# Writing the first stage's order by hand: TensorE, GpSimd and SyncE in program order, two recurrences interleaved

## The chip, the cores and the metric

The kernel runs on one core of one Trainium2 chip. The metric is device time in microseconds (us) of one execution, the median over several executions; lower is better. The engines of the core are named as the profile names them: PE is TensorE's matmul, PEld its weight loads, DVE is VectorE, ACT is ScalarE, POOL is GpSimd and SP is SyncE, which here only issues DMA transfers. An engine takes its instructions in the order in which they stand in its queue, so an instruction that waits holds back all that stand behind it on that engine.

## The reference

The reference is a two-layer decoder trunk on x of 1 x 1024 x 1024 in float32. Layer 0 mixes tokens with an HGRN2 gated recurrence, layer 1 with a causal convolution module; each is followed by a squared-ReLU MLP, and each of the four parts by a layer norm of the scaled residual. The change touches layer 0's mixer alone:

```python
proj = h @ w_in                                   # (S, 4D): q | forget | value | output gate
q, fz, v, g = jnp.split(proj, 4, axis=-1)
q = silu(q);  f = lb + (1 - lb) * sigmoid(fz);  k = 1 - f
# 8 heads of 128 x 128, chunkwise over time:
#   S_t = diag(f_t) S_{t-1} + k_t v_t^T,   o_t = S_t^T q_t
o = o * rsqrt(mean(o * o, -1) + RMS_EPS) * norm_g * silu(g)
mix = o @ w_out
```

## The kernel before

**Numbers and products.** Every large product is made of float32 operands cut into a high and a low part (ACT casts the high one, DVE subtracts to get the low one; `cut`, L348), so a product of two operands is three matmuls: high-high, high-low, low-high. On top of that the projections use a seven-product scheme for 2 x 2 blocks in place of eight. The products are numbered 1 to 7 and run in the order 1, 2, 6, 5, 7, 3, 4 (`ORDER`, L43). Each needs its own sum of input blocks and its own sum of weight blocks, called forms.

**The first stage** is layer 0's mixer up to the output projection, and has these parts.

- *Value products* (`v_products`, L399): seven products, each of four token tiles with 12 matmuls of 512 columns. The order in the program is 1, 2, 6, 5, 7, 3, 4. The forms of x and of the value weights are made in between by DVE, ACT and POOL from five buffers `x00` to `x11` and `t6`, and `a0` to `a3` and `s7`. Finished values go to `vd` in device memory (L397).
- *Pair products* (`pair_product`, L729): twelve pairs, `PAIRS` in L513. A "q" pair makes Q and the forget gate of one head, a "g" pair the output gates of two heads. A pair is seven products of 12 matmuls, so there are 12 x 7 x 12 = 1008 of them. `pair_load` (L515) brings a pair's weights in two transfers into the one buffer pair `r0`, `r1`, and `pair_forms` (L523) makes its seven weight forms: POOL adds the blocks (L532 to L539), ACT and DVE cut the sums into a ring `fs` of eight slots. The forms of pair p+1 are made while pair p is multiplied, and as soon as they are made `pair_load(p + 2)` is issued (L549).
- *Recurrences* (`recurrence`, L572): one for each head and half of the sequence, sixteen in all. Each one is a chain that goes back and forth between DVE and PE: DVE multiplies Q and K by running decay products (`grow`, L593) at seven levels, POOL makes a rescaled copy `kd` (L610), PE makes scores at these levels into PSUM, DVE merges them under masks (`put`), PE transposes K, then multiplies scores by values and carries the state over four blocks, with a DVE step between. ACT takes squares, POOL the power -1/2 of the mean square (`power_m_half`, L428), ACT scales, PE transposes, and the result is stored to `od` (L695). `recurrence` is a generator; each `yield` ends a step.
- *Gates*: `swish` (L701) multiplies on POOL; `gate_out` (L770) loads a head from `od`, multiplies it by its gate on POOL, and stores it to `zd`.
- *Output projection* (from L1007): eight products of 24 matmuls for each half, from tiles `oT`, which `gated` and `last_head` fill, and weights `wb` and `wa`.

**Weight sums for later.** The MLPs use the seven products too. The sums of blocks of `ffn_w2` are made during the first stage, entirely by transfers in device memory: `block_sums` (L489) issues on SP a tiny store that serves as a gate on a computed tile (L493) and two loads of 1 MB (L494, L495), and then on POOL's queue three accumulating transfers, each of which must wait until what it adds to has landed:

```python
nc.gpsimd.dma_start(out=v[:, 0:2], in_=w[:, 2:4], accum_op=ALU.add)                                  # L496
for i in (2, 3):
    nc.gpsimd.dma_start(out=v[:, i], in_=v[:, i - 1], accum_op=ALU.add, max_dma_last_dim=4096)       # L498
```

There are sixteen such sums. Each of the first two recurrences starts two of them, each of the next ten starts one (L684), all when its normed output is there; the last two run in layer 1.

**What sets the order.** The program emits the work in one order: after each pair product so many steps of the oldest recurrence (`advance`, L754; 16/7 a product, 24/7 in the second and the last pair), one recurrence at a time, then the gates that are ready. This emission order is a priority only. A planner simulates the engines and puts each engine's queue, those of PE, POOL and SP included, in the order in which, by its own cost model, instructions become ready. On the chip each queue then runs as it was written.

The loop over the pairs, L861 to L881, shortened:

```python
for p, (kind, j) in enumerate(PAIRS):
    forms = None if last else pair_forms(p + 1)
    for i in ORDER:
        if kind == "q" and i == 2:
            while recs and recs[0][0] <= j - 2:      # Q and K have four slots
                advance()
        pair_product(p, i, made.pop(0), st)          # twelve matmuls
        next(forms)                                  # one form of the next pair
        rate += (24 if p in (1, len(PAIRS) - 1) else 16) / 7
        while rate >= 1:
            rate = rate - 1 if advance() else 0.0    # one step of the oldest recurrence
        gate_some()
    if kind == "q":
        recs += [[j, 0, None], [j, 1, None]]
```

Most PE and DVE instructions are issued through a helper at L172, so the profile shows that line for them and they are told apart by their tiles: `ps<-vw,xf` is a value product, `ps<-xf,fs` a pair product, `qk`, `kd`, `at`, `state`, `v`, `ident,o` belong to recurrences, `wa,oT` and `wb,oT` to the output projection, `raw` is a pair's weight buffer and `s` its form 7, `ss` is the mean square, `sum_w` a weight sum.

Of the kernel before, what the change touches and what calls it, by code (L numbers as in the profile page):

```python
# [236 lines left out]
def body(ctx, tc, d, out):  # L237
# [100 lines left out]

    par = cst.tile([P, NPAR], F32, name="par")
# [7 lines left out]

    def cut(hi, lo, raw):  # L348
        nc.scalar.copy(out=hi, in_=raw)  # L349
        vector.tensor_tensor(out=lo, in0=raw, in1=hi.bitcast(F32), op=ALU.subtract)  # L350
# [4 lines left out]
    def form_v(i):  # L355
        at = {1: (80, 88), 2: (96, 104), 6: (192, 200), 5: (208, 96), 7: (192, 200), 3: (208, 184), 4: (192, 200)}[i]
        VS[i] = [view(kb, (2, 1024), F32R, "vw") for kb in at]
# [41 lines left out]
    def v_products(i):  # L399
        for t, parts in enumerate(v_form(i)):  # L400
            product(banks[:, 4 + t] if i in (2, 5, 3) else banks[:, t], parts, i in (1, 2, 5))
            v_out(i, t)

# [12 lines left out]
    products([banks[:, t] for t in range(NTB)], v_form(1))  # L416
    load_v(a2, 1, 0)
    load_v(a3, 1, 2)
    load_x(x01, 1, 0)
# [19 lines left out]
    pool_add(s7[:, 0], a0[:, 0], a2[:, 0])  # L439
    for j in range(2):  # L440
        if j:
            vector.tensor_tensor(out=s7[:, j], in0=a0[:, j], in1=a2[:, j], op=ALU.add)
        for o, x, y in ((a2, a2, a3), (a0, a2, a0)):
            if j:
                vector.tensor_tensor(out=o[:, j], in0=x[:, j], in1=y[:, j], op=ALU.add)
            else:
                pool_add(o[:, j], x[:, j], y[:, j])
    for k in range(4):
        vector.tensor_tensor(out=x00[:, k], in0=x00[:, k], in1=x01[:, k], op=ALU.subtract)
        vector.scalar_tensor_tensor(out=t6[:, k], in0=x00[:, k], scalar=-1.0, in1=x11[:, k], op0=ALU.mult, op1=ALU.subtract)  # L450
        cut_x(6, t6, (k,))
    cut_v(6, a0)
    v_products(2)

    cut_x(5, x00)
    cut_v(5, a2)
    for k in range(4):
        vector.scalar_tensor_tensor(out=x10[:, k], in0=t6[:, k], scalar=-1.0, in1=x10[:, k], op0=ALU.mult, op1=ALU.subtract)
        pool.tensor_tensor(out=x01[:, k], in0=x11[:, k], in1=x01[:, k], op=ALU.subtract)
    outs_v(5)  # L460
# [3 lines left out]
    cut_x(3, x11)  # L464
    outs_v(4)
    lg = par[:, LB : LB + H]
# [9 lines left out]
    pool_add(a1[:, 0], a0[:, 0], a1[:, 0])  # L476
    vector.tensor_tensor(out=a1[:, 1], in0=a0[:, 1], in1=a1[:, 1], op=ALU.add)
    v_products(5)

    cut_x(7, x01)  # L480
    cut_v(7, s7)
    v_products(7)
    cut_v(3, a1)
    cut_x(4, x10)


    sums = {}

    def block_sums(name, layer, c, after):  # L489

        t = sums[name, layer, c] = dram.tile([4, P, 1024], F32, name=f"sum_{name}{layer}{c}")
        v, w = t.rearrange("a p n -> p a n"), d[name][layer, c].rearrange("a p n -> p a n")
        nc.sync.dma_start(out=t[0:4:2, 0, 0:1], in_=after)  # L493
        nc.sync.dma_start(out=v[:, 0:2], in_=w[:, 0:4:2])  # L494
        nc.sync.dma_start(out=v[:, 2:4], in_=w[:, 0:2])  # L495
        nc.gpsimd.dma_start(out=v[:, 0:2], in_=w[:, 2:4], accum_op=ALU.add)  # L496
        for i in (2, 3):
            nc.gpsimd.dma_start(out=v[:, i], in_=v[:, i - 1], accum_op=ALU.add, max_dma_last_dim=4096)  # L498

    to_sum = [(*of, c) for of in (("w2", 0), ("w2", 1)) for c in range(NFC)]  # L500

    def form(name, layer, c, i):

        w, t = d[name][layer, c], sums[name, layer, c]
        return {1: w[0], 2: w[1], 6: t[2], 5: t[1], 7: t[0], 3: t[3], 4: w[3]}[i]


# [58 lines left out]
    def load_values(i):  # L566
        if i < 2 * H:
            h, half = divmod(i, 2)
            vts[i] = view(166, rows, F32, "v") if i == 2 * H - 1 else vs()
            nc.sync.dma_start(out=vts[i], in_=vd[h // 4][half][:, :, h % 4 * P : (h % 4 + 1) * P])  # L570

    def recurrence(h, half):  # L572
# [4 lines left out]
        state = carry if half else None  # L577
# [11 lines left out]
        def total(n):  # L589
            t = totals[n].rearrange("p (b s) -> p s b", s=2)  # L590
            mul(totals[2 * n], t[:, 0], t[:, 1])

        def grow(n, k=True):  # L593
            nb = HT // (2 * n)
            if not k:
# [38 lines left out]
        for n in (16, 32, 64):  # L634
# [9 lines left out]
            if n == 16:  # L644
                put(0, pd)
# [211 lines left out]
    for _ in forms:  # L857
        pass
# [698 lines left out]
```

## Time and profile before

| | |
|---|---|
| median of 3 executions | 2360.37 us (2360.34 to 2363.32) |
| the profiled execution | 2359.79 us, its span 2358.0 us |
| granted clock over the span | 0.951 |
| PE busy | 2169.4 us (92%) |
| DVE, ACT, POOL busy | 1466.4, 1040.2, 547.6 us |
| mean DMA rate | 216 GB/s |

A profile is one execution. Busy time is the time in which at least one instruction of an engine ran; matmuls are pipelined, so the time between the starts of two matmuls that follow each other is what one costs, and it is shorter than the mean duration that a group shows. The granted clock is the share of TensorE's full speed that the chip let it have. A wait is put down to the instruction, or the transfer, that ended it.

### The profile page before, as it was taken

Reading aid. Unit: us, or ns where it says so; the run is one execution under the profiler, and the core shown is the slowest. Engines: PE = TensorE matmul, PEld = TensorE weight load, DVE = VectorE, ACT = ScalarE, POOL = GpSimd, SP = SyncE. Lnnn points to the kernel's source line nnn. Section 1 sums busy time; section 2 is a strip of 40 time slices with the busy share of each in tenths; the row PEclk is TensorE's granted clock in tenths of the full one; section 3 lists DMA queues with packets and bytes.
Section 4 is the critical chain, followed back from the end, with each engine's and each line's share of the span. In section 5 each row is a group of like instructions: output and inputs, shape, how many; then the busy total and the mean of one; then the engine's idle time right before and its main releaser. Section 6 shows DMA issues by size and latency. Waiting matters only on the chain.

```text
span 2358.0 us, 27326 instructions
## 1 busy us (share of the span) xinstructions
PE 2169.4 (92%) x10056; PEld 1787.7 (76%) x10056; DVE 1466.4 (62%) x1938; ACT 1040.2 (44%) x1607; POOL 547.6 (23%) x458
## 2 busy tenths in 40 slices
PE   7996486786779999999999999999999999999998
PEld 5875365565668888888888888888887888888887
DVE  8584355373547776665665679978963654455446
ACT  5342132242421465555444447664854344343333
POOL 3242433343211000000000028937920100000001
PEclk8997788797889999999999999999999999999999
DMA  4317965756713377768999986556459598875552
GB/s 167 104 53 200 219 179 142 188 145 166 209 47 135 115 254 243 280 214 297 359 337 345 328 303 234 180 215 232 171 180 326 183 339 318 299 262 192 194 177 99
DMA packets 170951, 508.63 MB, mean 216 GB/s; under 512 B 16192, under 2 KB 45120, under 8 KB 169792
## 3 DMA queue, kind: packets, MB, share of 16 engines
q1 hardware_dynamic: 161856, 473.32, 57.3%
q0 software_dynamic: 8960, 33.56, 8.1%
q8 instruction: 79, 1.29, 0.2%
q14 instruction: 56, 0.46, 0.1%
HBM read 377.32 MB, written 196.61 MB: 243 GB/s over the span
## 4 chain that ended last, share of the span: by engine, by line
PE 68%; DMA 15%; DVE 6%; POOL 5%; issue 3%; ACT 2%; SPq 0%; DVEq 0%; POOLq 0%
PE ps L172 68%; DMA sum_w<-in_w_dram 4%; DMA raw<-in_wqf_dram 3%; POOL cb L172 2%; DVE qk L172 2%; DMA raw<-in_w_dram 1%; DMA sum_w<-sum_w 1%; DMA y<-kept 1%; DMA wa<-ready 1%; DVE fs L172 1%; DMA vr<-in_wv_dram 1%; DMA dh<-hf 1%; POOL ss L429 1%; DMA raw<-in_wg_dram 1%; POOL kd L172 1%
## 5 line engine op out<-in xcount | busy, mean ns | idle before, releaser
L172 PE MATMUL ps<-dw,dh 128*128 128x512 f32 x2688 | 611.3, 389 | 0.5 <-ACT dh L69 0.5
L172 PEld LDWEIGHTS ps<-dw,dh 128*128 128x128 f32 x2688 | 504.1, 188 | 105.4 <-ACT dh L69 0.9
L172 PE MATMUL ps<-x1f,fw 128*128 128x512 f32 x1344 | 307.9, 390 | 1.0 <-DVE c L172 1.0
L172 PEld LDWEIGHTS ps<-x1f,fw 128*128 128x128 f32 x1344 | 251.4, 188 | 53.1 <-issue 1.4
L172 PE MATMUL ps<-xf,fs 128*128 128x512 f32 x1008 | 269.5, 427 | 21.2 <-ACT t L736 19.5
L172 PE MATMUL ps<-xa,wa 128*128 128x512 f32 x1152 | 268.8, 392 | 0.0
L172 PEld LDWEIGHTS ps<-xf,fs 128*128 128x128 f32 x1008 | 205.7, 208 | 69.8 <-ACT t L736 21.1
L172 PEld LDWEIGHTS ps<-xa,wa 128*128 128x128 f32 x1152 | 214.3, 188 | 43.5
L172 POOL TENSOR_TENSOR cb<-cb,prod 128x512 f32<-128x512 f32 x176 | 234.2, 1340 | 17.7 <-ACT prod L1325 7.2
L172 DVE TENSOR_TENSOR dh<-dh 128x1024 fp32r<-128x1024 f32 x112 | 136.4, 1222 | 118.9 <-ACT dh L69 117.0
L172 DVE SCALAR_TENSOR_TENSOR ps<-u,par,ps 128x512 f32<-128x512 f32 x288 | 198.7, 750 | 9.8 <-ACT ps L1337 8.4
L429 POOL TENSOR_TENSOR mv<-mv,nhalf 128x1 f32<-128x1 f32 x32 | 47.4, 1483 | 655.5 <-DVE mv L172 655.5
L172 DVE TENSOR_TENSOR dw<-dr,dw 128x1024 fp32r<-128x1024 f32 x112 | 136.6, 1222 | 100.8 <-ACT dw L69 100.4
L69 ACT CAST dh<-dh 128x1024 fp32r<-128x1024 f32 x112 | 117.0, 1051 | 150.0 <-DMA dh<-hf 147.0
L69 ACT CAST dw<-dr 128x1024 fp32r<-128x1024 f32 x112 | 117.4, 1053 | 132.1 <-PE ps L172 115.1
L172 PE MATMUL ps<-xc,wa 128*128 128x512 f32 x768 | 174.4, 389 | 0.0
L172 PEld LDWEIGHTS ps<-xc,wa 128*128 128x128 f32 x768 | 144.1, 188 | 29.9
L1325 ACT ACTIVATE prod<-u,par 128x512 f32<-128x512 f32 x176 | 125.3, 722 | 54.0 <-POOL cb L172 53.4
L1190 POOL COPY next<-ss 128x1 f32<-128x1 f32 x37 | 15.9, 429 | 488.5 <-DVE spare L172 235.1
L172 DVE TENSOR_TENSOR qk<-qk,T 128x512 f32<-128x512 f32 x96 | 73.0, 762 | 89.4 <-PE ps L172 53.4
L349 ACT CAST fs<-raw 128x512 fp32r<-128x512 f32 x72 | 44.0, 619 | 173.6 <-POOL raw L172 67.5
L172 DVE TENSOR_TENSOR fs<-raw,fs 128x512 fp32r<-128x512 f32 x72 | 64.6, 902 | 87.5 <-ACT fs L349 86.9
(193 smaller groups left out, 2986.7 us busy)
## 6 DMA issues: line engine op xcount, KB each, us to landing
wa<-ready SPq DMA_DIRECT2D x122, 512.0 KB
dh<-hf SPq DMA_DIRECT2D x112, 512.0 KB
ready<-spare SPq DMA_DIRECT2D x74, 512.0 KB
sum_w<-in_w_dram SPq DMA_DIRECT2D x32, 1024.0 KB
dr<-sum_w SPq DMA_DIRECT2D x64, 512.0 KB
raw<-in_w_dram SPq DMA_DIRECT2D x51, 512.0 KB
dr<-in_w_dram SPq DMA_DIRECT2D x48, 512.0 KB
raw<-in_w1q_dram SPq DMA_DIRECT2D x36, 512.0 KB
```

What stands on the lines that cost most here:

```text
L69: self.nc.scalar.copy(out=slot[:, 0, c], in_=raw[:, c])
L172: return op(*args, **kw)
L349: nc.scalar.copy(out=hi, in_=raw)
L429: nc.gpsimd.tensor_tensor(out=dst, in0=src, in1=nhalf[:, :n], op=ALU.pow)
L1190: nc.gpsimd.tensor_copy(out=raw[:, :1], in_=now)
L1325: nc.scalar.activation(tp, u[:, k : k + HT], AF.Copy, scale=tap(j, k))
```

## The change

PE, POOL and SP leave the planner for the whole first stage: their queues run in the order in which the program emits the work (`tc.manual_schedule`). DVE and ACT stay with the planner, and so does everything after the stage. The emission order is rewritten to go with it:

- The value products run in the order 1, 2, 5, 6, 7, 3, 4, with the forms made right ahead of each; `x01` is loaded ahead of `a2` and `a3`.
- A clock of ticks is kept: one tick after every three matmuls of a pair product or of the early output products, four after a tile of a value product. `later(n, job)` emits a job n ticks later. A weight sum's two loads are emitted at once, its three accumulating transfers 24, 48 and 72 ticks later.
- The first four sums start in value products 5, 6, 7 and 3, one in each; the first ten recurrences start one each. As before, two are left for layer 1.
- A pair product is emitted in quarters of three matmuls. After each quarter, from the second pair on, 222/308 of a recurrence step is emitted. Two recurrences are under way at a time: the next starts when the one before has made seven of its fourteen steps. The state updates and the last steps are spread over more steps than before, and the state passes between the halves of a head through `carry`, kept by head.
- `kd` and the product in Q's swish go from POOL to DVE. In the g pairs the swish of a copied gate stays on POOL.
- The forms are made at most five products ahead, in a ring of six slots in place of eight; Q and K get six slots in place of four.
- A gate's multiplication on POOL is emitted six ticks after its load is issued.
- At the end of the stage three output products, (0,0), (1,0) and (2,0), are made in the last steps of the last recurrence; the five others of the first half follow after the stage, in another order than before.

The core of the diff:

```diff
+    order = ExitStack()
+    order.enter_context(tc.manual_schedule(engines={mybir.EngineType.PE, mybir.EngineType.Pool, mybir.EngineType.SP}))
...
+    def later(n, job):
+        if n:
+            waiting.append((ticks[0] + n, job))
+        else:
+            job()
+
+    def tick(n=1):
+        for _ in range(n):
+            ticks[0] += 1
+            for at, job in [w for w in waiting if w[0] <= ticks[0]]:
+                waiting.remove((at, job))
+                job()
...
+    def block_sums(name, layer, c, after, gap=0):
...
+        nc.sync.dma_start(out=t[0:4:2, 0, 0:1], in_=after)
+        nc.sync.dma_start(out=v[:, 0:2], in_=w[:, 0:4:2])
+        nc.sync.dma_start(out=v[:, 2:4], in_=w[:, 0:2])
+        parts = [lambda: nc.gpsimd.dma_start(out=v[:, 0:2], in_=w[:, 2:4], accum_op=ALU.add)]
+        for i in (2, 3):
+            parts.append(lambda i=i: nc.gpsimd.dma_start(out=v[:, i], in_=v[:, i - 1], accum_op=ALU.add, max_dma_last_dim=4096))
+        for i, part in enumerate(parts):
+            later((i + 1) * gap, part)
...
     def v_products(i):
...
             v_out(i, t)
+            if t == 0 and i in (5, 6, 7, 3):
+                block_sums(*to_sum.pop(0), VO[{5: 5, 6: 6, 7: 5, 3: 6}[i]][0][:2, :1], 24)
+            tick(4)
...
     def recurrence(h, half):
...
-        pool.tensor_tensor(
-            out=kd.rearrange("p a (b n) -> p a b n", n=4), in0=B.rearrange("p a (b n) -> p a b n", n=4),
-            in1=cutout(rm, 0, [[P, 2], [1, P], [0, 4]]), op=ALU.mult,
-        )
+        mul(kd.rearrange("p a (b n) -> p a b n", n=4), B.rearrange("p a (b n) -> p a b n", n=4), cutout(rm, 0, [[P, 2], [1, P], [0, 4]]))
...
-        for _ in range(2 if 2 * h + half < 2 else 1 if 2 * h + half < 12 else 0):
-            block_sums(*to_sum.pop(0), o[:2, 0, :1])
+        if 2 * h + half < 10:
+            block_sums(*to_sum.pop(0), o[:2, 0, :1], 24)
+        yield
         yield
...
-            pool.tensor_tensor(out=out, in0=t, in1=sg, op=ALU.mult)
+            (vector if out is not t else pool).tensor_tensor(out=out, in0=t, in1=sg, op=ALU.mult)
...
     def pair_product(p, i, f, st):
...
+        for k in range(4):
...
+            tensor.matmul(ps, lh, rh, start=i in (1, 2, 5) and k == 0, stop=False, **group)
+            tensor.matmul(ps, lh, rl, start=False, stop=False, **group)
+            tensor.matmul(ps, ll, rh, start=False, stop=k == 3, **group)
+            if k < 3:
+                slot()
...
+        slot()
...
+    def step():
+        if recs and (not active or len(active) == 1 and active[0][2] >= 7):
+            at = recs.pop(0)
+            active.append([at, recurrence(*at), 0])
+        if not active:
+            return False
+        one = active[0]
+        if len(active) == 2 and active[0][2] - active[1][2] > 7:
+            one = active[1]
+        one[2] += 1
...
+    def slot():
+        tick()
+        pace[0] += pace[1]
+        while pace[0] >= 1:
+            pace[0] = pace[0] - 1 if step() else 0.0
...
+        pending.append(rest)
+        later(6, lambda: pending and pending[0] is rest and pending.pop(0)())
...
     for p, (kind, j) in enumerate(PAIRS):
...
+        pace[1] = 222 / 308 if p else 0.0
...
+    early_out = ((0, 0), (1, 0), (2, 0))
+    for (t, n), ps in zip(early_out, (banks[:, i] for i in range(3))):
+        for k, ((lh, ll), (rh, rl)) in enumerate(wide(oT[0], t, ws[n])):
...
+            tick()
+            if k % 2:
+                step()
+    while step():
+        pass
+    gated(1, range(H - 2))
     last_head(1)
+    tick(100)
...
+    order.close()
```

283 lines of the change are left out of this document (131 added, 152 removed).

## The prediction

> **What bounds the kernel now.** I read the slices of the page first, to see where TensorE (PE) is idle, then the chain that ended last, then tables by stage, then the groups and waits of the stage.
>
> ```profile
> span 2358.0 us, 27326 instructions
> PE   7996486786779999999999999999999999999998
> PEclk8997788797889999999999999999999999999999
> PE 68%; DMA 15%; DVE 6%; POOL 5%; issue 3%; ACT 2%; SPq 0%; DVEq 0%; POOLq 0%
> ```
>
> A slice is 59 us. Slices 3 to 12 are ragged in both rows, everything after is 9: the loss lies in the first stage, to about 712 us. A fifth of the chain is DMA and GpSimd (POOL), engines that should hide.
>
> ```profile
> 50.00:75.00 25.00, 25.00 (x112) 20.69 (x111) 17.62 (x29) 12.65 (x20) 0.00 (x0) 1.00 0.08 23
> 97.00:712.00 615.00, 453.47 (x2343) 368.63 (x2342) 326.43 (x536) 188.18 (x431) 208.29 (x158) 0.83 0.59 150
> 125.00:175.00 50.00, 46.08 (x224) 36.74 (x225) 43.48 (x66) 19.86 (x35) 21.88 (x15) 0.97 0.14 43
> 712.00:850.00 138.00, 137.04 (x663) 114.17 (x662) 104.91 (x149) 50.59 (x87) 12.86 (x9) 1.00 0.40 140
> 91.78 5.60 PE L172 MATMUL ps<-vw,xf 128*128 128x512 f32 x24
> 97.22 3.11 PE L172 MATMUL ps<-xf,fs 128*128 128x512 f32 x13
> ```
>
> The stretch table gives PE, weight loads, VectorE (DVE), ScalarE (ACT) and POOL busy, granted clock, DMA share, GB/s; below are two rows of the timeline. The value (V) products end and the pair products begin at 97. From 97 to 712 (615 us) PE is busy for 453 at a clock of 0.83; after 712 it is busy for 137 of 138. At full clock PE takes 25.00 / 112 = 0.223 us per 512-column matmul. Its real work in the 615 us follows from the groups:
>
> ```profile
> L172 PE MATMUL ps<-xf,fs 128*128 128x512 f32 x1008 | 269.5, 427 | 21.2 <-ACT t L736 19.5 <-DVE t L172 1.0 <-DVE fs L172 0.4
> L172 PE MATMUL ps<-qk 128*128 128x128 f32 x256 | 44.9, 331 | 21.2 <-DVE qk L172 14.6 <-ACT on L691 6.5
> L172 PE MATMUL ps<-wa,oT 128*128 128x512 f32 x49 | 16.3, 469 | 2.7 <-ACT wa L69 1.9 <-DVE wa L172 0.8
> L172 PE MATMUL ps<-ident,o 128*128 128x128 f32 x60 | 14.3, 361 | 51.1 <-ACT o L683 51.1
> L172 PE MATMUL ps<-wb,oT 128*128 128x512 f32 x48 | 13.0, 402 | 3.2 <-DVE oT L172 2.7 <-DVE t L172 0.6
> L172 PE MATMUL ps<-qk 128*32 128x32 f32 x256 | 7.5, 204 | 7.0 <-DVE qk L172 7.0
> 640.18 1.05 PE L172 MATMUL ps<-qk 128*128 128x128 f32 x8
> 648.73 0.45 PE L172 MATMUL ps<-qk 128*32 128x32 f32 x16
> 654.98 0.68 PE L172 MATMUL ps<-qk 128*64 128x64 f32 x8
> ```
>
> Pair products: 1008 x 0.223 = 225 us. Recurrences: seven 128-column groups, from x256 to x56, hold 852 matmuls at 1.05 / 8 = 0.131, so 112; 256 narrow ones at 0.45 / 16 make 7, 128 half-wide ones at 0.68 / 8 make 11; together 130. The 97 output-projection matmuls already inside are 22. That is 377 us of work in 615: **238 us are lost to waits and half clock**, the most the change can win there. Who causes the waits:
>
> ```profile
> L498 POOL DMA_DIRECT2D sum_w<-sum_w x28 | 24.0, 858 | 125.5 <-DMA sum_w<-in_w_dram 80.0 <-DMA sum_w<-sum_w 45.5
> L496 POOL DMA_DIRECT2D sum_w<-in_w_dram x14 | 17.2, 1230 | 95.3 <-DMA sum_w<-in_w_dram 51.2 <-issue 35.6 <-PE ps L172 8.5
> L172 POOL TENSOR_TENSOR s<-raw 128x512 f32<-128x512 f32 x11 | 15.4, 1400 | 39.2 <-DMA raw<-in_wqf_dram 33.9 <-DMA raw<-in_wg_dram 5.3
> 118.61 3.98 DMA raw<-in_wqf_dram
> 194.36 18.65 DMA raw<-in_wqf_dram
> 225.51 26.33 DMA raw<-in_wqf_dram
> 271.38 11.39 DMA sum_w<-in_w_dram
> 283.12 6.21 DMA sum_w<-sum_w
> ```
>
> POOL stands still for 80.0 + 51.2 + 45.5 = 177 us until a weight sum's transfer lands, and behind it in its queue stand the adds that make the next pair's weight forms, kd, and the power step of the norm. The last five rows, from the chain, show the same in order of time: a pair's weights take 3.98 us on a quiet DMA, 18.65 and 26.33 behind sums.
>
> **The change, part by part.**
>
> *Sums in late steps.* Each of 14 sums has two loads on SyncE's (SP) queue and three accumulating transfers on POOL.
>
> ```profile
> q1 hardware_dynamic: 34547, 80.05, 33.3%
> q0 software_dynamic: 7840, 29.36, 23.4%
> sum_w<-in_w_dram POOLq DMA_DIRECT2D x14, 1024.0 KB, 10.3
> sum_w<-sum_w POOLq DMA_DIRECT2D x28, 512.0 KB, 5.5
> ```
>
> The accumulates are now emitted 24, 48 and 72 ticks after the loads; a tick is three pair matmuls plus their share of recurrence, (225 + 130) / 336 = 1.06 us of PE (1008 / 3 = 336), so 24 ticks are 25 us, and among V products (tick(4) per twelve matmuls) 24 x 12 x 0.223 / 4 = 16 us. Both exceed the landing of 10.3 and 5.5, so the 177 us of POOL waits go; issuing, 24.0 + 17.2, stays. Four sums move from the first two recurrences into the V products, where the DMA share was 0.08 (50 to 75 us), so no more than one sum follows a recurrence. Bytes stay the same: (33.3% + 23.4%) of the 720 us window is 408 us of all 16 engines, still under the new length of the stage.
>
> [...]
>
> *What is late next: pair loads.* Forms run five products ahead (the ring goes from eight slots to six), so a load issued then has 5 x 4 x 1.06 = 21 us until PE needs it. Behind at most one sum instead of two I take the smaller loaded row, 18.65, as the likely latency. PE hides that; POOL and ACT don't, as in their queues the first add and cast wait for it, with the norm's power step behind. One product (4 x 1.06 = 4.2 us) passes before they reach the load, and a further 10 us I estimate to be covered by the second recurrence and by products already formed: 18.65 - 4.2 - 10 = 4 us for each of 11 pairs, **44 us**. Bounds: 0 (a quiet load, 3.98) and 26.33 - 4.2 - 10 = 12 each, 133.
>
> *Work moved from POOL to DVE.*
>
> ```profile
> L172 POOL TENSOR_TENSOR kd<-qk,rm 128x1024 f32<-128x1024 f32 x16 | 36.0, 2251 | 56.6 <-PE ps L172 44.0 <-DVE T L172 12.5
> L172 POOL TENSOR_TENSOR qk<-t,sq 128x512 f32<-128x512 f32 x16 | 23.8, 1488 | 15.2 <-PE ps L172 8.6 <-ACT sq L704 6.5
> L172 DVE TENSOR_TENSOR vw<-vr,vw 128x1024 fp32r<-128x1024 f32 x12 | 15.6, 1298 | 5.7 <-ACT vw L349 5.6
> L172 DVE TENSOR_TENSOR t<-t,ps 128x512 f32<-128x512 f32 x24 | 16.4, 681 | 23.7 <-PE ps L172 15.2 <-ACT t L736 8.5
> ```
>
> kd and the swish product of Q leave POOL (59.8 us less) and cost DVE 16 x 1.298 + 16 x 0.681 = 32. DVE then has 326 + 32 = 358 us in a stage where PE has 371 (225 + 130, and 16 of the tail below): the engines are nearly even, and DVE, which every recurrence step waits for, sets the pace. DVE's fullest stretch above is 43.48 of 50 us, 0.87, while PE did 46.08: so the stage takes 358 / 0.87 = **412 us** with nothing else late. Bounds: PE's own 371 at 46.08 / 50, that is 403; and 358 at the 0.76 of 712 to 850 (104.91 / 138), 471.
>
> *Hand order on PE, two halves alternating.* After every three pair matmuls PE takes 222/308 of a recurrence step, from two recurrences half a length apart, and two more slots of Q and K keep a third head's halves ready. The waits of the old order
>
> ```profile
> PE ps L172 <- ACT o L683: 51.1, 8, 16.8
> PE ps L172 <- DVE qk L172: 50.0, 44, 5.1
> ```
>
> get other work between step and step. But PE can no longer go round a late step: what waits for DVE now holds the pair products as well. That is inside the 0.87, not extra.
>
> *SP in program order.* Behind a store that waits for ACT or for a landing stand the next pair load, value load and sum loads:
>
> ```profile
> SPq L570 <- PE ps L172: 125.1, 11, 25.7
> SPq L772 <- DMA od<-on: 41.3, 6, 16.8
> ```
>
> SP waited there already, through the value ring of three and the gates; emission now follows PE's order, so I count nothing beyond the 44 us. If a gate's re-load finds its store not yet landed, SP stands for 16.8 at worst, once for each of three gate pairs, 50 in all.
>
> *The V products*, from the stretch table:
>
> ```profile
> 0.00:97.00 97.00, 81.63 (x336) 65.77 (x336) 70.14 (x83) 43.12 (x66) 28.52 (x23) 0.93 0.43 152
> ```
>
> Their order and first loads change, PE's busy time stays. I take 0. Bounds: 10 us less, of the 15 in which PE isn't busy, or 10 more, one accumulate's landing (10.3), if the sums delay the first pair load.
>
> *Tail.* Three output products, 72 x 0.223 = 16 us, run between the last steps; before, 97 such matmuls (22 us) were done by 712. So 6 us of work are left over.
>
> *The sum.* Pair stage 412 + 44 = 456, against 615. Gain 615 - 456 - 6 = 153 us. The profiled execution took 2359.79 (span 2358.0), 0.6 below the median of 2360.37, so the two stand for each other: 2359.8 - 153 = **2206**.
>
> Granted clock: the sum prices PE at full clock. [...]
>
> **The rivals.**
>
> *B, loads stay late (0.20).* Sums now overlap all the time instead of in bursts, and every pair load meets one. For: the 18.65 and 26.33 rows. Against: 118.61, 3.98 us, and only 408 us of DMA. Without the 10 us of cover each of the 11 loads costs 18.65 - 4.2 = 14; with it and the longer row, 12. I take 13: 143 in all, a stage of 412 + 143 = 555 and a gain of 615 - 555 - 6 = 54, so 2306.
>
> *C, PE sets the pace (0.13).* Loads hide, and DVE fits under PE: a stage of 403, the lower bound above, a gain of 615 - 403 - 6 = 206, so 2154. For: 43.48 us of DVE went with 46.08 of PE in one stretch. Against: fixed order makes PE wait wherever DVE is late.
>
> *D, slower (0.08).* POOL still waits out each accumulate, since the loads land after 24 ticks, and PE, now in fixed order, waits along. Price: (10.3 + 2 x 5.5) x 14 = 298 on top of 412 makes a stage of 710, against 615 and with the 6 us of the tail 101 more: 2461. It decides once a load-to-accumulate gap of 16 to 25 us is shorter than the landing; at 10.3 that is far, at 26.33 it is reached. The part that PE does go round today, 177 + 39 us of POOL waits in 238 lost, speaks for its size.
>
> *E, no difference (0.02).* The planner's order was already the written one. Speaks against it: POOL's own queue waits 177 us on what the text moves away.
>
> **How the numbers follow.** My forecast has 0.57. Faster by over 0.2% (5 us, about what this measurement can tell from nothing) is 0.57 + 0.20 + 0.13 = 0.90; within it 0.02; slower 0.08. The range runs from 2150, a little below C, to 2320, past B: it leaves out D and E (0.10), B's upper quarter (0.05) and C's lower third (0.04).
>
> **What would show it.** Right: sum_w's waits on POOL under 40 us; PE's busy share from 97 to the end of the pairs over 0.85, clock over 0.9; DVE over 0.8 there; pair products end near 540; waits on "DMA raw" between 30 and 60 us; DMA share about 0.75. Wrong: POOL waiting for sums over 100 us (D), ACT or POOL waiting for raw over 100 (B), DVE under 0.75 without any DMA behind it, or a hole after 553 where the output products wait for y.

## The result and the profile after

| | before | changed |
|---|---|---|
| median of 4 executions | 2361.32 us (2360.34 to 2363.32) | 2262.73 us (2259.18 to 2266.18) |
| the profiled execution | 2359.79 us | 2262.96 us |
| its granted clock over the span | 0.951 | 0.973 |

The ratio is 0.9581 [0.9565, 0.9598]: 99 us less, where 153 were forecast. The time lies inside the range, between the forecast (2206) and the rival of late loads (2306). From the page of the changed kernel come the slices of PE and of its clock and the shares of the chain:

```profile
span 2261.2 us, 27315 instructions
PE   7969878598999999999999999999999999999998
PEclk8979989798999999999999999999999999999999
PE 75%; DMA 9%; DVE 7%; POOL 4%; issue 2%; ACT 2%; SPq 0%; DVEq 0%; POOLq 0%; ACTq 0%
```

The ragged stretch ends two slices earlier, and the chain's DMA share falls from 15% to 9%. Everything that was gained lies in the first stage: its recurrences' last state product came at 711.8 us before and comes at 601.8 now. Of these 110 us some 12 are given back behind the stage, since 44 output matmuls are done by then and not 97 (53 x 0.223). The stretch table from the start of the pairs to there (columns as in the prediction), then two quarters of its start:

```profile
97.00:602.00 505.00, 400.35 (x2297) 328.74 (x2296) 328.27 (x564) 183.56 (x431) 160.11 (x128) 0.90 0.63 169
100.00:125.00 25.00, 14.93 (x57) 11.91 (x58) 5.10 (x7) 7.37 (x13) 7.46 (x9) 0.84 1.05 257
125.00:150.00 25.00, 11.36 (x47) 9.05 (x45) 18.98 (x33) 8.93 (x15) 8.61 (x8) 0.77 0.89 208
```

The work in these 505 us is 225 + 130 us of pairs and recurrences and 44 output matmuls (10), 365 in all, so 140 us are lost, against 238 before and 85 in the forecast (371 in 456). The clock rose from 0.83 to 0.90. DVE is busy for 0.65 of the stage, not 0.87. In the two quarters at the start the DMA share is 1.05 and 0.89, and PE is busy for 14.93 and 11.36 of 25 us. Some groups of the stage, and one row of its waits:

```profile
L376 POOL DMA_DIRECT2D sum_w<-sum_w x27 | 25.6, 957 | 32.7 <-issue 31.5 <-DMA sum_w<-sum_w 1.2
L374 POOL DMA_DIRECT2D sum_w<-in_w_dram x12 | 14.9, 1240 | 2.6 <-DMA vd<-vo 2.6
L172 POOL TENSOR_TENSOR s<-raw 128x512 f32<-128x512 f32 x11 | 16.9, 1536 | 88.1 <-DMA raw<-in_wqf_dram 33.1 <-DMA raw<-in_wg_dram 20.8 <-DVE fs L172 19.3
L389 ACT CAST fs<-raw 128x512 fp32r<-128x512 f32 x70 | 42.7, 620 | 134.9 <-PE ps L172 70.5 <-DMA raw<-in_wg_dram 26.2 <-POOL raw L172 17.0
L172 DVE TENSOR_TENSOR kd<-qk,rm 128x1024 f32<-128x1024 f32 x16 | 24.6, 1540 | 0.3 <-PE ps L172 0.3
L172 DVE TENSOR_TENSOR qk<-t,sq 128x512 f32<-128x512 f32 x16 | 12.7, 795 | 2.0 <-ACT sq L710 2.0
L172 DVE TENSOR_TENSOR qk<-qk,f 128x512 f32<-128x512 f32 x32 | 23.4, 731 | 0.2
ACT fs L389 <- DMA raw<-in_wqf_dram: 17.0, 4, 7.7
```

The sums' 177 us of waits on POOL are 35 (1.2 + 2.6 for landings, 31.5 under "issue", which means that the profile shows nothing that POOL waited for); one more of 10.4 us lies in the value products, ahead of this window. What is late now is what was named as next: POOL waits 33.1 + 20.8 us for a pair's weights, ACT 26.2 + 17.0, 97 in all. The chain of waits by line, for each kernel from 97 us to its own last recurrence, shows the exchange; the first row is before, cut off where the view cuts it, the second the changed kernel.

```profile
by line: PE ps L172 19.0%; DMA sum_w<-in_w_dram 16.0%; DMA raw<-in_wqf_dram 10.2%; issue 9.3%; DVE qk L172 7.0%; DMA sum_w<-sum_w 3.6%; DVE fs L172 2.7%; POOL ss L429 2.0%; DMA raw<-in_wg_dram 2.0%; POOL kd L172 2.0%; DVE T L172 1.7%; POOL 
```

```profile
by line: PE ps L172 34.6%; DMA raw<-in_wqf_dram 9.9%; DVE qk L172 9.2%; DMA raw<-in_wg_dram 6.5%; issue 6.4%; DMA u<-od 4.4%; DVE fs L172 3.5%; DMA vd<-vo 3.5%; DVE kd L172 3.0%; DVE at L172 1.7%; ACT fs L389 1.6%; POOL raw L172 1.6%; DVE T
```

Waits for the sums (16.0% and 3.6%) no longer stand in the chain. Loads of pair weights and gates and the store of V took 9.9 + 6.5 + 4.4 + 3.5 = 24.3% of 505 us, 123 us. Some of their pieces (start, us):

```profile
102.78 17.55 DMA vd<-vo
227.53 12.13 DMA raw<-in_wqf_dram
267.73 12.36 DMA raw<-in_wqf_dram
317.38 12.63 DMA raw<-in_wg_dram
348.93 14.89 DMA raw<-in_wqf_dram
380.27 15.16 DMA u<-od
438.93 15.21 DMA raw<-in_wg_dram
```

A pair's weights, 3.98 us at 118.61 before (DMA share 0.21 from 100 to 125 us), take 12 to 15 in five of the seven pieces (10.48 and 5.19 in the two others).

### The profile page after: what moved, and what is told of

The parts are those of the page before. It is cut to its first block, busy times and chain, and to the rows that moved or that the text cites. A ratio compares the mean times of both kernels' runs of the same rounds, so it can differ in the third digit from the quotient of the medians.

```text
span 2261.2 us, 27315 instructions
## 1 busy us (share of the span) xinstructions
PE 2129.0 (94%) x10056; PEld 1758.2 (78%) x10056; DVE 1471.6 (65%) x1970; ACT 1034.0 (46%) x1607; POOL 492.6 (22%) x426
## 4 chain that ended last, share of the span: by engine, by line
PE 75%; DMA 9%; DVE 7%; POOL 4%; issue 2%; ACT 2%; SPq 0%; DVEq 0%; POOLq 0%; ACTq 0%
PE ps L172 75%; POOL cb L172 3%; DMA raw<-in_wqf_dram 2%; DVE qk L172 2%; DMA raw<-in_wg_dram 1%; DMA vd<-vo 1%; DMA u<-od 1%; DMA wa<-ready 1%; DMA raw<-in_w_dram 1%; DVE fs L172 1%; DVE kd L172 1%; DMA vr<-in_wv_dram 1%; DVE at L172 0%; ACT fs L389 0%; POOL raw L172 0%
## 5 line engine op out<-in xcount | busy, mean ns | idle before, releaser
L172 PE MATMUL ps<-xf,fs 128*128 128x512 f32 x1008 | 287.7, 425 | 27.5 <-ACT t L752 25.7
L172 PEld LDWEIGHTS ps<-xf,fs 128*128 128x128 f32 x1008 | 188.6, 200 | 63.3 <-ACT t L752 26.7
L172 PE MATMUL ps<-qk 128*128 128x128 f32 (+2 forms) x640 | 60.8, 256 | 59.9 <-DVE qk L172 51.7
L172 PEld LDWEIGHTS ps<-qk 128*128 128x128 f32 (+2 forms) x640 | 54.5, 167 | 78.8 <-issue 39.5
L172 DVE TENSOR_TENSOR wa<-raw,wa 128x1024 fp32r<-128x1024 f32 x55 | 71.3, 1299 | 67.6 <-ACT wa L69 67.5
```

The source lines that it names most:

```text
L172: return op(*args, **kw)
```

## The experiments

All were measured beside the kernel before on the same chip. Chips differ by some us (the kernel before came to 2358.94, 2361.80 and 2365.60 us on three of them), so kernels are compared by the ratio to before; 0.001 of it is 2.4 us.

| kernel | median us | ratio [95%] |
|---|---|---|
| changed | 2262.73 | 0.9581 [0.9565, 0.9598] |
| without the accumulates | 2203.05 | 0.9341 [0.9325, 0.9358] |
| accumulates at once | 2342.13 | 0.9922 [0.9905, 0.9939] |
| no sums in the V products | 2262.29 | 0.9585 [0.9566, 0.9605] |
| second load of a sum later | 2246.32 | 0.9521 [0.9507, 0.9535] |
| kd and swish back on POOL | 2298.03 | 0.9726 [0.9706, 0.9747] |
| one recurrence at a time | 2284.57 | 0.9670 [0.9651, 0.9688] |
| planner orders, emission kept | 2253.21 | 0.9532 [0.9507, 0.9557] |
| sums placed behind the pair loads | 2208.62 | 0.9342 [0.9322, 0.9363] |
| the same, planner orders | 2358.79 | 0.9986 [0.9972, 1.0001] |
| the same, recurrences start later | 2207.65 | 0.9334 [0.9300, 0.9369] |
| changed, PE alone to the planner | 2276.58 | 0.9637 [0.9616, 0.9659] |
| before, with the new sums alone | 2363.75 | 0.9999 [0.9985, 1.0013] |

My theory after the result: what is missing of the forecast is lost to the accumulates' traffic, which the pair and gate loads meet; POOL and ACT wait for those in their queues, DVE behind them, and PE in its fixed order. Rivals: DVE sets the pace; the hole at the start of the pairs is the loss; the fixed order of PE is.

**Without the accumulates.** In the first stage the three accumulating transfers of each sum are left out, so its value isn't made; the loads stay.

```diff
-        for i, part in enumerate(parts):
-            later((i + 1) * gap, part)
+        parts.clear() if gap else [part() for part in parts]
```

> The changed kernel (2262.7 us) with the three accumulating transfers of every first-stage weight sum left out, so the sums stay incomplete and the output is not the reference's; the loads of the sums stay. My theory: what kept the gain at 99 us in place of 153 is transfers that land late (pair loads, gate re-loads, value stores behind the sums), since TensorE is idle for 105 us of the 499 from 97 to 596 and the chain of that stretch shows 12 to 15 us at each pair load. The accumulates are 163 us of all 16 DMA engines out of some 400, so without them I expect 2210 to 2230 and GpSimd's 32 us of standing before an accumulate gone. Rival: the fixed order on TensorE waits for the VectorE chain of each recurrence whatever the transfers do; then the time stays within 10 us of 2263 and the waits on DVE qk stay at 56 us.

It came to 0.9341, a little more than I expected: the accumulates cost 0.024, 57 us, all of what was missing. The stretch table to the last recurrence, and the chain by line there:

```profile
97.00:541.00 444.00, 387.43 (x2307) 318.98 (x2306) 320.51 (x563) 181.90 (x428) 121.85 (x87) 0.95 0.38 128
```

```profile
by line: PE ps L172 46.9%; DVE qk L172 9.0%; DMA raw<-in_wqf_dram 6.2%; issue 6.2%; DVE fs L172 3.3%; DVE kd L172 2.4%; DMA vd<-vo 2.4%; DVE T L172 2.2%; DMA raw<-in_wg_dram 2.1%; DVE at L172 2.0%; ACT fs L388 1.6%; POOL ss L471 1.5%; POOL 
```

The four kinds of transfer fall from 24.3% of 505 us to 10.7% of 444 us (no u<-od is left among those shown), 47 us. DVE's work, 320.5 us, is nearly that of the changed kernel (328.3), and its share still only 0.72. The run also spares POOL the issuing of the accumulates (25.6 + 14.9 us) and the 35 us of waits, so by itself it doesn't separate the traffic from POOL's queue; the run with the sums behind the pair loads does, further below.

**Accumulates at once.** The three follow the loads without ticks.

```diff
-                block_sums(..., 24)        # both places
+                block_sums(..., 0)
```

> The changed kernel with the gap of 24 ticks set to 0: the three accumulates of a sum are emitted right behind its loads, as before the change; the rest of the hand order stays. My theory: the late steps carry most of what GpSimd won; at once, GpSimd waits again for the landings (177 us in 14 sums before), now with TensorE held by the fixed order, so 60 to 110 us slower than 2263, 2320 to 2370. Rival D of the prediction in its full size: GpSimd's 298 us all come through, 2450 and more. Other rival: TensorE is held by late pair loads anyway and the sums' own waits fall beside them; then less than 20 us slower.

It came to 0.9922: under the hand order the late steps are worth 0.034, 80 us. POOL's waits to the last recurrence:

```profile
POOL sum_w L376 <- DMA sum_w<-in_w_dram: 122.0, 12, 11.8
POOL sum_w L374 <- DMA sum_w<-in_w_dram: 82.6, 10, 9.1
POOL sum_w L376 <- DMA sum_w<-sum_w: 75.5, 13, 10.5
```

280 us, close to the 298 at which the rival "slower" was priced; but the time rose by only 80.

**No sums in the V products.** The four sums go to recurrences 11 to 14.

```diff
-            if t == 0 and i in (5, 6, 7, 3):
+            if False:
...
-        if 2 * h + half < 10:
+        if 2 * h + half < 14:
```

> The changed kernel with no sum in the value products; recurrences 11 to 14 start one each in their place, so there are still 14. My theory: the sums in the value products cost the start of the pairs about 25 us (TensorE does 22.8 us of work between 100 and 150; the chain there is value stores of 11.8 and 17.6 us and pair loads of 4.8 and 10.5). Without them the pairs begin without a hole, minus 20 to 25 us; the four sums moved add some 5 us each to later pairs, so 2243 to 2263 in all, and the 9 us idle at 112 us is gone. Rival: the hole at the start is the recurrence chain's own start-up on VectorE (the 13.6 us that end at 149); then the start stays as it is and the time rises by 5 to 20 us.

No difference, 0.9585. PE waits for a pair's copied sum (`ACT t`) twice, 19.9 us, where it was three times and 25.7, the 9.2 us near 112 among them; and the stage gives it back: POOL waits 65.9 us for gate loads (39.3 in the changed kernel) and 48.4 for g weights (20.8). The hole at the start is a place where the loss shows, not the loss.

```profile
POOL u L172 <- DMA u<-od: 65.9, 8, 16.7
POOL s L172 <- DMA raw<-in_wg_dram: 48.4, 3, 17.6
```

**The second load of a sum later**, by half the gap:

```diff
-        nc.sync.dma_start(out=v[:, 2:4], in_=w[:, 0:2])
+        later(gap // 2, lambda: nc.sync.dma_start(out=v[:, 2:4], in_=w[:, 0:2]))
```

> The changed kernel with the second 1 MB load of each sum emitted 12 ticks after the first, not right behind it. My theory: pair loads and gate re-loads are late because 2 MB stand ahead of them in one queue; with 1 MB at a time they come 3 us sooner, and the 11 pair loads and 12 gate re-loads give 10 to 30 us: 2233 to 2253. Rival: it is the total of the transfers that fills the engines, not their clumping; then within 5 us of 2263.

0.9521, 14 us faster with the same bytes, as my theory had it.

**kd and the swish of Q back on POOL.**

```diff
-        mul(kd..., B..., cutout(...))
+        pool.tensor_tensor(out=kd..., in0=B..., in1=cutout(...), op=ALU.mult)
...
-            (vector if out is not t else pool).tensor_tensor(...)
+            pool.tensor_tensor(...)
```

> The changed kernel with kd and the product in Q's swish back on GpSimd, everything else as changed. My theory, after the run without accumulates came out at 2203, where the prediction stood: VectorE sets the pace once the transfers are out of the way, but with them it is busy for only 0.65 of the stretch, so giving it 32 us less helps little, while GpSimd, which waits for transfers in its queue, gets kd into every recurrence's chain (2.25 against 1.5 us, and whatever stands ahead of it): 15 to 40 us slower than 2263. Rival, from the prediction's sum: VectorE's busy time over 0.87 is the stage, then 32 / 0.87 = 37 us faster, 2226.

0.9726, 34 us slower. PE's waits for DVE's products rise from 56.0 to 106.9, although DVE has less to do. What changed shows on POOL, which now stands 35.8 us in five waits ahead of `kd` and 80.8 us in fourteen ahead of Q's swish, where the changed kernel has neither on POOL; how much of it DVE and PE wait for isn't traced. So the rival of DVE's busy time fails here. As the work went to POOL, into every recurrence's chain, this run alone doesn't show what less work for DVE would bring; that DVE is busy for only 0.65 of the stage speaks against it as well.

```profile
PE ps L172 <- DVE qk L172: 106.9, 18, 15.8
```

**One recurrence at a time.**

```diff
-        if recs and (not active or len(active) == 1 and active[0][2] >= 7):
+        if recs and not active:
```

> The changed kernel with one recurrence under way at a time: the next starts only when the one before has ended; steps and pace stay. My theory: the fourteen steps of one chain then follow each other at 1.45 us of TensorE's time, where a step needs 2 to 4 us of VectorE and back, so TensorE, in fixed order, waits some 1 to 2 us at most of the 224 steps, less what VectorE's slack hides: 60 to 150 us slower, 2320 to 2410. Rival: the alternation matters little, as TensorE is held by late transfers anyway: within 20 us of 2263.

0.9670: the alternation is worth 0.009, 21 us, about what the rival had and less than I expected. Some of the waits that it takes away can be named: those for `o` and the state, 8.5 and 2.6 us in the changed kernel, come back.

```profile
PE ps L172 <- ACT o L689: 27.0, 13, 8.2
PE ps L172 <- DVE state L172: 21.6, 7, 5.5
```

**The planner orders the new emission.** The line with `manual_schedule` is dropped.

> The changed kernel with the hand order taken off: the same emission, but the planner orders TensorE, GpSimd and SyncE by its own cost model, as before the change. My theory: the new emission (four sums early, three accumulates spread, alternation) is only a priority to the planner, which issues an accumulate as soon as it believes that its loads have landed; GpSimd's waits for sums come back in part, 50 to 150 us of them, and the time lies between, 2290 to 2340. Rival: the emission is the whole of it and the planner keeps it: within 10 us of 2263. Other rival: the planner goes round late steps and does better than the fixed order: under 2250.

0.9532, about 12 us *faster* than the hand order (the two intervals just don't meet); my theory, 2290 to 2340, is missed. POOL waits for sums again:

```profile
POOL sum_w L375 <- DMA sum_w<-sum_w: 61.4, 10, 9.3
POOL sum_w L375 <- DMA sum_w<-in_w_dram: 57.8, 9, 9.7
POOL sum_w L373 <- DMA sum_w<-in_w_dram: 34.6, 8, 9.2
```

That is 154 us, nearly the 177 of before, in a kernel 110 us faster than before. So a kernel can have those waits and be as fast: that they go is not by itself what the change saved.

**Sums placed behind the pair loads.** Eleven sums start right behind a pair load, when POOL and ACT have their weights under way and the next pair load is a whole pair off, about 38 us (453 / 12); their accumulates follow after 10, 20 and 30 ticks; three stay in V products 2, 5 and 6; none hangs on a recurrence. Bytes are the same.

```diff
             pair_load(p + 1)
+            block_sums(*to_sum.pop(0), None, 10)     # None: no gating store
...
-        if 2 * h + half < 10:
-            block_sums(*to_sum.pop(0), o[:2, 0, :1], 24)
...
-            if t == 0 and i in (5, 6, 7, 3):
+            if t == 0 and i in (2, 5, 6):
```

> The changed kernel with the sums started by the pair loads: three in the value products 2, 5 and 6, and one right behind the transfers of each of the eleven later pair loads, its accumulates 10, 20 and 30 ticks later; none in the recurrences. A pair load then meets no sum ahead of it, as the sum before it has had a whole pair (28 ticks, 38 us) to get through. My theory: late pair loads are most of what the transfers cost, so 25 to 45 us faster than 2263: 2218 to 2238, and waits on raw on GpSimd and ScalarE, 97 us in the changed kernel, under 40. Rival: the gate re-loads and value transfers that now meet the sums cost the same again: within 10 us of 2263.

0.9342, 56 us faster than the changed kernel, more than I expected, and level with the one that leaves the accumulates out. The waits of POOL and ACT for a pair's weights fall from 97 us to 37 (19.2 + 3.9 and 7.8 + 5.8). The stretch table, and the medians from issue to landing of the transfers over the whole execution, first the changed kernel, then this one (tile, queue, count, KB each, us):

```profile
97.00:550.00 453.00, 387.23 (x2284) 319.72 (x2284) 320.64 (x562) 180.92 (x426) 149.85 (x122) 0.92 0.68 182
```

```profile
sum_w<-in_w_dram SPq DMA_DIRECT2D x32, 1024.0 KB, 7.2
raw<-in_wqf_dram SPq DMA_DIRECT2D x16, 512.0 KB, 7.0
raw<-in_wg_dram SPq DMA_DIRECT2D x8, 512.0 KB, 13.7
u<-od SPq DMA_DIRECT2D x12, 256.0 KB, 12.7
```

```profile
sum_w<-in_w_dram SPq DMA_DIRECT2D x32, 1024.0 KB, 10.1
raw<-in_wqf_dram SPq DMA_DIRECT2D x16, 512.0 KB, 5.5
raw<-in_wg_dram SPq DMA_DIRECT2D x8, 512.0 KB, 4.3
u<-od SPq DMA_DIRECT2D x12, 256.0 KB, 10.4
```

The DMA engines are busy for as long as in the changed kernel (0.68 x 453 = 308 us, 0.63 x 505 = 318), yet the pair loads land sooner (13.7 to 4.3, 7.0 to 5.5), gate re-loads a little (12.7 to 10.4), and the loads of the sums, which PE doesn't need in this stage, later (7.2 to 10.1). POOL's waits for the sums don't shrink, they are 50 us (26.9 + 12.4 for landings, 11.0 at "issue") against 35. So it isn't the amount of traffic that costs the 56 us, nor POOL's waits for the sums, but what the traffic meets. The run changes three things at once, the place of the sums, their gating stores and their ticks (10 for 24), and doesn't tell them apart. The stores alone are not a likely cause: SP stands 130.1 us at them in the changed kernel, but the run without accumulates keeps all ten of the recurrences' and is as fast (0.9341).

**The same with the planner.**

> The sums stand right behind each pair load, as in the aligned run (2208.62), and the planner orders the engines in place of the hand order. Theory (the emission does the work, not the order; with the hand order off the kernel changed came to 2253.21 against 2262.73): the planner gives a little here too, about 2200, between 2190 and 2215, and GpSimd's waits for the sums come back to some 100 to 150 us without costing time. Rival (the fixed order pays once no load is late, since it keeps the accumulates off GpSimd's way): 2225 to 2250, with the sums' waits on GpSimd's path.

No faster than before, 0.9986, and both expectations missed. Without a gating store nothing but the fixed order holds the loads of eleven sums back, and the planner moves them to the front: the last of the first loads starts at 140.0 us, against 468.4 under the hand order. The stretch table, up to 350 us, and PE's longest waits:

```profile
0.00:97.00 97.00, 60.71 (x240) 48.32 (x240) 58.25 (x67) 34.45 (x52) 24.12 (x21) 0.86 1.01 308
97.00:350.00 253.00, 107.25 (x497) 85.18 (x498) 78.80 (x127) 44.59 (x73) 60.57 (x56) 0.70 0.80 189
```

```profile
PE ps L172 <- ACT fs L389: 106.6, 3, 79.8
PE ps L172 <- ACT xf L389: 55.6, 2, 54.4
```

The DMA share is 1.01 up to 97 us and 0.80 from there to 350, and PE waits once for 79.8 us and once for 54.4 us. So the place of these loads in SP's queue can cost as much as the whole change gained. The run doesn't tell what the planner would make of these sums if something held them back.

**The same with later recurrences** in the second pair, by two products:

```diff
-        pace[1] = 222 / 308 if p else 0.0
         for i in ORDER:
+            pace[1] = 222 / 300 if p > 1 or p and i in ORDER[2:] else 0.0
```

> The aligned run, with the recurrence steps of the second pair's first recurrences beginning eight slots later, so that the first of them does not meet the first pair load's DVE work. Theory (the hole of about 10 us near 130 us comes from TensorE waiting in its fixed order for the first recurrence's DVE chain): the hole goes and the time is 2199, between 2193 and 2205. Rival (a hole filled at the start is given back later, as the run without the V-product sums showed): 2206 to 2213, TensorE's idle time in the stage unchanged within 5 us.

0.9334, no difference that can be told. The longest wait for `qk`, 9.8 us, is now 5.8; the idle time of PE from 97 to 640 us stays at 65 us, where it was 66. So a hole made smaller at the start came back elsewhere.

**PE alone to the planner.** The hand order stays on POOL and SP.

```diff
-    order.enter_context(tc.manual_schedule(engines={mybir.EngineType.PE, mybir.EngineType.Pool, mybir.EngineType.SP}))
+    order.enter_context(tc.manual_schedule(engines={mybir.EngineType.Pool, mybir.EngineType.SP}))
```

> The kernel changed, with the hand order kept on GpSimd and SyncE's queue only; TensorE's order goes to the planner. Theory (the order on TensorE is neither gain nor loss, the planner's gain of 9.5 came from GpSimd's and the queue's order): 2258 to 2266, as the kernel changed. Rival (the fixed order of TensorE costs, since it waits in it for late recurrences): 2245 to 2255, as with the planner on all three, and DVE waits on TensorE's path below 56 us.

0.9637, 13 us slower than the changed kernel; neither theory had it. The waits for `qk` halve (28.8, none over 2.5 us), but others take their place: PE now waits 23.5 us for forms. A likely reading, not shown: POOL, in its own fixed order, makes them later than the planner thinks.

```profile
PE ps L172 <- DVE qk L172: 28.8, 27, 2.5
PE ps L172 <- ACT fs L389: 23.5, 10, 6.2
```

**Before, with the new sums alone**: four in the V products, ten in the recurrences, accumulates emitted 24, 48 and 72 ticks later, four ticks a product; the planner orders all.

> The kernel before, planner and head order untouched, with the sums' emission alone changed: four started in V products, ten in recurrences, and the three accumulates of each emitted 24, 48 and 72 steps later. Theory (late steps need neither the hand order nor the alternation to take GpSimd's waits of 177 us for the sums away): these waits fall under 100 us and the time to about 2305, between 2285 and 2325, what is left being the alternation (22) and the work moved to DVE (35). Rival (the planner moves the accumulates forward again, or the head-after-head order leaves them no place): waits above 150 us and 2345 to 2365, no gain.

0.9999: nothing. The rival is right, and the rows of the tile `sum_w` say how. In each pair of rows (first and last start) are a sum's second load and its first accumulate, here and then in the changed kernel:

```profile
L371 SPq DMA_DIRECT2D sum_w<-in_w_dram x14: 591/610/2937, 57.3 to 540.2; - x14
L372 POOL DMA_DIRECT2D sum_w<-in_w_dram x14: 1190/1236/1399, 63.1 to 546.3; - x14
```

```profile
L373 SPq DMA_DIRECT2D sum_w<-in_w_dram x14: 600/612/1493, 50.5 to 436.4; - x14
L374 POOL DMA_DIRECT2D sum_w<-in_w_dram x14: 1162/1224/1447, 56.3 to 460.7; - x14
```

In the last sum the first accumulate starts 6.1 us behind the load under the planner, 24.3 under the hand order: to the planner a late emission is a priority only, and it hands POOL the accumulate at once. Late steps without the hand order are no late steps.

## Why the prediction came out as it did

The direction and the place were right. Of the 57 us between 2206 and 2262.96, the recurrences' end accounts for 49 (601.8, forecast 553) and the tail for 6 (44 instead of 72 output matmuls were done by then, 28 x 0.223).

- **The POOL waits go: right, but read too simply.** They fell from 177 to 35 us; under the hand order late steps are worth 80 us. The spacing among the value products was wrong: ticks order POOL's own queue but don't tie it to PE. The first two sums' first accumulates start 5.8 and 6.2 us behind their second loads, not 16, and nine of the twelve accumulates of the four early sums are issued from 101 to 142 us, beside the pairs and not in the quiet value products. With the planner, though, 154 us of such waits stood in a kernel as fast as this one, and the new sums alone brought nothing to the kernel before. A likely reading, not shown by itself: the planner gives PE other work to go round POOL's waits, the fixed order doesn't, and so needs the late steps. The parts don't add up one by one: late steps 80, work to DVE 34, alternation 21, hand order -12, together 123 against 99. The hand order gained nothing with these sums; with the sums behind the pair loads it is what holds them there (2208.62 against 2358.79).
- **Late pair loads, 44 us: the term that was mis-sized.** "Behind at most one sum" was the wrong count: a sum's two loads can stand ahead of the next pair load on one queue and the last of its accumulates comes 72 ticks later, and the DMA share is 0.63 over the stage. And the term priced pair loads alone, while gate loads (15.16 on the chain), the store of V (17.55) and POOL's own issuing (31.5 us) were late too. With the accumulates out, or placed behind the pair loads, the stage loses 79 or 88 us (444 or 453 us less 365), where the changed kernel loses 140 and the forecast had 85. What was missing, 55 us, has the size of what these runs give back (61 and 52). What late transfers cost in all isn't shown, as 47 us of them are left on the chain without the accumulates.
- **DVE at 0.87: fell.** No run had it above 0.73 over the stage, 0.72 even where the accumulates are out and the DMA share is 0.38; and moving work from DVE back to POOL cost 34 us. What made 412 look sound is that two errors offset each other: DVE's own work came out smaller (320.5 us without the accumulates, not 358; `qk<-qk,f` takes 731 ns in the changed kernel, 1119 before, in the rows of the stage), and its share lower: 320.5 / 0.72 is 444. `kd` and the swish cost 1540 and 795 ns, not 1298 and 681: 37 us for 32. That the run without accumulates and the one with the sums behind the pair loads end at 2203 and 2209, beside the forecast of 2206, is therefore luck in the terms and doesn't confirm them.
- **SP's order, 0: the weak point.** Moving the sums in that queue, with their stores and ticks, decides 56 us. Gate re-loads stand on the chain with two pieces, 15.16 + 7.19, inside the bound of 50.
- **PE can't go round a late step: right, at a price.** The 13.6 us at 135.8, for `qk`, are such a wait. (The 9.2 us at 112 are not: a pair product waits there for a copy on ACT, which stands behind a form that waited 13.3 us for a landing.) But to free PE alone was worse by 13.
- **Value products, 0.** Pairs start at 100.8 us instead of 97.2: inside the bound of 10.
- **Granted clock.** It rose from 0.83 to 0.90 in the stage, to 0.92 with aligned sums and to 0.95 without accumulates. Around the 13.6 us from 135.8 on in which PE stood, it was 1.00 from 135 to 140 us, 0.57 from 140 to 145, 0.50 from 145 to 150, 0.57 from 150 to 155 and 1.00 from 155 to 160. Before, it was 0.50 from 210 to 220 us, with PE busy for 2.69 of these 10: the half clock among the 238 us. What the lower clock costs beside the idle time itself, the runs can't part.
- **Loads beside the sums.** Loads of a q pair, issued by SP, land after 7.0 us beside POOL's accumulates and after 4.1 without them. With the sums behind the pair loads, those of a g pair land after 4.3 us instead of 13.7, with the same bytes in the sums: where the sums stood in the order changed what the other loads took.
- **The rivals.** "Loads stay late" had the mechanism, at somewhat over half its size (57 of the 100 us from 2206 to 2306). "POOL waits out each accumulate" is real at gap 0, as 80 us. "PE sets the pace" (2154) was reached by no run.
- **The signs.** Only sum_w's waits came out as written, 35 us and under 40. From 97 to the end of the pairs, at 586 and not near 540, PE is busy for 0.79 (over 0.85 was expected) at a clock of 0.90 (just the limit); DVE for 0.65, not over 0.8; the DMA share is 0.63, not 0.75; and the waits for raw, 97 us on POOL and ACT together, stand just below the 100 that were to speak for "loads stay late". By these signs the result lies nearer to that rival than to the forecast.

What stays open: which of the other parts (six form slots, the rewritten steps, work moved, alternation) makes up the 110 us by which the new emission beats the old sums-only kernel under the planner; only the hand-ordered versions of two of them were taken out. The traces of these two runs differ where `kd` has left POOL: with the old emission POOL stands 29.1 us ahead of it from 97 to 600 us. ACT stands 65.8 us for POOL's pair adds in the kernel before, from 97 to 712 us, and 23.1 with the new emission under the planner, from 97 to 640. That is a lead, not a test.

## What to carry to other kernels

Here, transfers that nobody waits for were cheap only where they did not hold up loads that somebody waits for: without the sums' accumulates the ratio is 0.9341, with the sums right behind a pair load 0.9342, and with the sums hung on value products and recurrences 0.9581. So start background traffic right behind the critical load, where it has the whole time until the next one. The fixed order took waits out only with the slow steps emitted late by hand as well: POOL stood for the sums for 35 us with late steps and for 280 without. This planner doesn't keep a late emission: in the last sum the first accumulate started 6.1 us behind the load under the planner, in the kernel before with the new sums, and 24.3 under the hand order. A busy share taken from one good stretch, 0.87, is no bound for a stage, which no run had above 0.73; test whether an engine sets the pace by giving it less work, and not by handing the work to an engine on the same chain.

## What was not expected of the hardware

An accumulate on POOL stood at "issue" though what it adds should have landed long before. The third row below is, by the emission order, the last accumulate of the first sum, whose second was issued at 71.17; the longest landing of a sum's transfer up to 700 us is 16.1 us. In the changed kernel's timeline (start, us, instruction, idle before it):

```profile
101.27 1.16 POOL L374 DMA_DIRECT2D sum_w<-in_w_dram  x1
102.01 1.32 POOL L376 DMA_DIRECT2D sum_w<-sum_w  x1
114.57 0.82 POOL L376 DMA_DIRECT2D sum_w<-sum_w  x1 [11.23 <-issue]
```

A 1 MB and a 512 KB accumulate were issued right ahead of it, and it starts 13.3 us after the first of them; the 1 MB ones land after 12.4 us in the median. Four such waits add up to the 31.5 us. In the run with aligned sums three of 512 KB were issued in a row without such a wait:

```profile
95.63 2.49 POOL L377 DMA_DIRECT2D sum_w<-sum_w  x3
```

What held the one in the changed kernel back isn't shown; no run tested it. And a larger DMA share went with a faster kernel (0.68 and 0.9342, against 0.63 and 0.9581): the busy time is about the same, only the stage is shorter, so the share by itself says little.
